# Three edits in the state-space rounds of a one-core hybrid trunk: where a second output row is scaled, how many rows the meta tokens' state product has, and which PSUM bank one output step uses

## The chip, the core and the metric

The kernel runs on one core of a Trainium2 chip. The metric is the device time of one execution in microseconds (us); lower is better. TensorE (PE in the profile, its weight loads PEld) multiplies matrices into PSUM, VectorE (DVE), ScalarE (ACT) and GpSimd (POOL) work element by element, SyncE (SP) issues transfers. Each engine runs its own list of instructions in the order of the list and waits on semaphores for what the others produce. PSUM has eight banks of 128 rows by 512 float32; a matmul writes into one of them.

## The reference

One layer of a hybrid decoder: RMS norm, one wide input projection, a pooling branch and a Mamba-2 branch, their gated sum, an output projection, an MLP and a final norm. 512 tokens are processed behind 16 learned meta tokens, with 1024 channels. The part that matters here is the Mamba-2 branch:

```python
xbc = jax.nn.silu(causal_depthwise_conv(xbc, conv_w, conv_b))     # x, B and C, width 4
dt = jax.nn.softplus(dt_raw + dt_bias);  a = -jnp.exp(a_log)
...
y_diag = jnp.einsum("bclsg,bclsgr,bcsgrp->bclgrp", cb, lmat, xdt)
states = jnp.einsum("bclgn,bclgr,bclgrp->bcgrpn", bf, decay_states, xdt)
...                                                               # states carried from chunk to chunk
y_off = jnp.einsum("bclgn,bcgrpn,bclgr->bclgrp", cf, prev, jnp.exp(a_cs))
y = (y_diag + y_off) + xs * d_skip[:, None]
y = y.reshape(bsz, seqlen, D_INNER) * jax.nn.silu(z)
yg = yg * lax.rsqrt(jnp.mean(yg * yg, axis=-1, keepdims=True) + EPS)   # over each of 8 groups
y_ssd = (yg * norm_w) @ w_ssd_out
```

The 16 meta tokens are a chunk of their own in front of four chunks of 128 tokens. There are 8 groups of 4 heads, 64 channels per head and 128 states.

## The kernel before

Everything is kept transposed: channels lie on the 128 partitions, tokens along the free axis. A float32 product is made of three float32r products (high by high, high by low, low by high), so each weight block of 128x1024 is loaded by SP, copied to a high half `whi` on ACT (L75) and its rest `wlo` taken on DVE (L76). Activations such as the branch's output are split in the same way, into `yh` (ACT, L542) and `yl` (DVE, L543).

The Mamba-2 branch runs in eight rounds g = 0 to 7, one per group. In a round the scan of group g (class `Scan`) is interleaved with four "steps" of PE work that keep TensorE filled (`scan_with`, L601 to L638). In rounds 0 to 3, 5 and 6 the steps are the projections of the next group: the B tile, the C tile and the two x tiles (`xbc_tile`), each followed by its convolution (`conv`, L344: one ACT instruction L347 and three DVE instructions L350). In round 4 they are the first half of the output projection (`out_half`), in round 7 its second part (`out_part`, L593): eight products `psp0` to `psp7` of six k-tiles each, added to `acc` by DVE (L597). The order inside the rounds is the order of the code for PE, ACT and DVE (`tc.manual_schedule`, L640); the program sets the waits.

A round, in the order of the code: `turn` transposes B and x on PE (tiles `ptb`, `ptx`, `ptm`) and forms `btok`, `xdt`, `xdd` and the meta tokens' operands `bm` and `xm`; then the step of PE work and its convolution; `spread` (ACT, L457: `eb`); `states` (PE: `pcb`, `pst`; ACT: `st` L486; DVE: `cbm`, `st` L488 and L489); second step; `spans` and `decays` (ACT, L463 and L468 on `abc`); third step; `spans`, `decays`, `scores` (DVE, L493); `outputs` (PE: `po` L503, `py` L509); then `gather`, `squares`, `norm`, `root` and `finish`, which scales the group's output rows by the norm and splits them.

Three places are touched.

*Second rows.* `finish` handles two rows of 128 channels. Where no gate product follows the round (rounds 0 and 5), the second row of group g is left for the next round: `rows.append(sc)`, and `scan_with` does it after the B tile's convolution and `spread` (L608). So it stands in rounds 1 and 6 only. Its three instructions are the multiply `yt` (DVE, L539), the cast `yh` (ACT, L542) and the rest `yl` (DVE, L543).

*Meta rows.* `bm` and `xm` hold the high parts, the rests and again the high parts at partitions 0, 32 and 64, with zeros between, in tiles of `MQ` = 80 partitions that are zeroed once (L140, L142). One float32r matmul over 80 rows (L485) is the meta chunk's state.

*PSUM.* Of the eight banks, four make up two double tiles (`psum2`, two buffers, used by projections and the output steps) and four are single tiles (`psum1`). In round 7 the first step is two products in a row (`two`, L644), both in double tiles. Ahead of them the two double buffers held `pz7` and the gate product `pgp6`; ACT reads `pgp6` for the sigmoid `m1` (L674), which was put in `held` and is issued after `turn`.

## Time and profile before

| | |
|---|---|
| median of three runs | 1012.45 us (1012.41 to 1012.48) |
| the profiled execution, its own time | 1012.34 us |
| its span, first to last instruction | 1010.5 us |
| PE / PEld busy | 999.8 us (99%) / 871.5 us (86%) |
| DVE busy | 712.3 us (70%) |
| ACT busy | 560.6 us (55%) |
| POOL busy | 88.7 us (9%) |
| granted TensorE clock | 0.999 |
| rounds 0 to 7 of the branch | about 66 to 475 us of the span |

Times in rows are us from the span's start, then the duration in us, the engine, the line, the operation and its tiles (out<-in), shapes and the number of merged instructions; a bracket gives the time the engine stood idle before it and who ended that. In a list of waits the columns are the total in us, how often, and the longest. The hardware pipelines instructions, so a row may begin some hundredths before the row ahead of it has ended. Buffer numbers are left out of tile names.

### The profile page before, as it was taken

To read this page: it belongs to the slowest core of one execution; us is meant where nothing else is said; L and a number is where in the kernel's file an instruction comes from. 1 tells how busy PE (TensorE), PEld (TensorE's weight loads), DVE (VectorE), ACT (ScalarE), POOL (GpSimd) and SP (SyncE) were. 2 spreads that over 40 slices of the span, in tenths; PEclk is the share of its full clock that TensorE was granted. 3 is DMA by queue.
4 is the path that set the end of the run, shared out by engine and by line. 5 is a ranking of instruction groups with operands and counts; after the bars stand their busy time and mean duration, and the time that the engine had idled before them with its cause. 6 is when DMAs were issued, how large, how long until landed. Compare 5 with 4: busy or idle time off the path is not lost.

```text
span 1010.5 us, 14027 instructions
## 1 busy us (share of the span) xinstructions
PE 999.8 (99%) x5689; PEld 871.5 (86%) x5689; DVE 712.3 (70%) x894; ACT 560.6 (55%) x789; POOL 88.7 (9%) x52
## 2 busy tenths in 40 slices
PE   9999999999999999999999999999999999999997
PEld 8889989898889999888898888888888888888886
DVE  7978687776745677677766557885766677666866
ACT  7756958595843659574244333465545455354444
POOL 0100000000000000000000001003040431412400
PEclk9999999999999999999999999999999999999999
DMA  6232232323232232324533234042323323324112
GB/s 242 71 142 104 64 125 84 120 73 131 75 127 90 76 119 70 132 78 133 179 105 95 94 104 177 10 161 90 104 91 117 104 84 125 104 84 126 42 42 84
DMA packets 29281, 105.62 MB, mean 105 GB/s; under 512 B 3296, under 2 KB 4256, under 8 KB 28192
## 3 DMA queue, kind: packets, MB, share of 16 engines
q1 hardware_dynamic: 26496, 92.75, 27.1%
q0 software_dynamic: 2000, 11.08, 2.8%
q8 instruction: 44, 0.72, 0.3%
q10 hardware_dynamic: 720, 0.91, 0.3%
q14 instruction: 21, 0.17, 0.1%
HBM read 102.55 MB, written 2.16 MB: 104 GB/s over the span
## 4 chain that ended last, share of the span: by engine, by line
PE 84%; DVE 7%; ACT 7%; issue 1%; DMA 0%; SPq 0%; DVEq 0%; ACTq 0%
PE pf L99 6%; PE pf L100 6%; PE pf L101 6%; PE px L157 3%; PE px L158 3%; PE px L160 3%; PE alpha L1071 3%; PE alpha L1072 3%; PE alpha L1073 3%; PE pz L160 2%; PE pz L157 2%; PE pz L158 2%; PE pp L157 2%; PE pp L160 2%; PE pp L158 2%; PE pso L99 1%
## 5 line engine op out<-in xcount | busy, mean ns | idle before, releaser
L76 DVE TENSOR_TENSOR wlo<-raw,whi 128x1024 fp32r<-128x1024 f32 (+1 forms) x131 | 163.9, 1252 | 111.8 <-ACT whi L75 111.5
L75 ACT CAST whi<-raw 128x1024 fp32r<-128x1024 f32 (+1 forms) x131 | 135.9, 1040 | 124.0 <-PE pf L100 55.7
L157 PE MATMUL px<-uh,whi 128*128 128x264 f32 (+1 forms) x448 | 118.9, 286 | 0.0
L158 PE MATMUL px<-ul,whi 128*128 128x264 f32 (+1 forms) x448 | 117.5, 283 | 0.0
L99 PE MATMUL pf<-vh,whi 128*128 128x512 f32 x256 | 99.8, 390 | 0.0
L101 PE MATMUL pf<-vh,wlo 128*128 128x512 f32 x256 | 99.6, 389 | 0.0
L100 PE MATMUL pf<-vl,whi 128*128 128x512 f32 x256 | 99.6, 389 | 0.0
L160 PE MATMUL px<-uh,wlo 128*128 128x264 f32 (+1 forms) x448 | 90.4, 283 | 0.0
L157 PEld LDWEIGHTS px<-uh,whi 128*128 128x128 f32 x448 | 84.8, 189 | 1.3 <-issue 1.0
L158 PEld LDWEIGHTS px<-ul,whi 128*128 128x128 f32 x448 | 84.4, 188 | 0.0
L833 DVE TENSOR_TENSOR slo<-b,shi 128x1024 fp32r<-128x1024 f32 x35 | 49.2, 1405 | 31.6 <-ACT shi L832 27.4
L160 PEld LDWEIGHTS px<-uh,wlo 128*128 128x128 f32 x448 | 68.8, 188 | 0.0
L832 ACT CAST shi<-b 128x1024 fp32r<-128x1024 f32 x35 | 36.8, 1050 | 47.3 <-PE pf L100 36.4
L101 PEld LDWEIGHTS pf<-vh,wlo 128*128 128x128 f32 x256 | 48.1, 188 | 10.1
L99 PEld LDWEIGHTS pf<-vh,whi 128*128 128x128 f32 x256 | 48.1, 188 | 9.9
L100 PEld LDWEIGHTS pf<-vl,whi 128*128 128x128 f32 x256 | 48.1, 188 | 9.9
L1082 POOL TENSOR_TENSOR b<-b,b 128x1024 f32<-128x1024 f32 x14 | 35.6, 2541 | 238.3 <-DVE slo L833 238.3
L1071 PE MATMUL alpha<-shi,hh 128*128 128x512 f32 x140 | 54.6, 390 | 0.0
L1073 PE MATMUL alpha<-shi,hl 128*128 128x512 f32 x140 | 54.5, 389 | 0.0
L1072 PE MATMUL alpha<-slo,hh 128*128 128x512 f32 x140 | 54.5, 389 | 0.0
L898 DVE TENSOR_TENSOR ht<-ht,alpha 128x1024 f32<-128x1024 f32 x35 | 42.6, 1217 | 10.9 <-PE alpha L1073 10.9
L157 PE MATMUL pz<-uh,whi 128*128 128x512 f32 x112 | 43.7, 390 | 0.0
(418 smaller groups left out, 2476.6 us busy)
## 6 DMA issues: line engine op xcount, KB each, us to landing
raw<-in_w SPq DMA_DIRECT2D x129, 512.0 KB, 3.5
b<-in_w SPq DMA_DIRECT2D x28, 512.0 KB, 3.5
abc<-acs_d POOLq DMA_DIRECT2D x8, 1024.0 KB, 5.3
wob<-in_w SPq DMA_DIRECT2D x8, 512.0 KB, 5.0
xt<-in_xT SPq DMA_DIRECT2D x8, 264.0 KB, 5.1
ht<-in_x POOLq DMA_DIRECT2D x4, 512.0 KB, 7.2
w<-in_w SPq DMA_DIRECT2D x4, 512.0 KB, 3.5
out_dram<-out SPq DMA_DIRECT2D x4, 320.0 KB, 2.4
```

Of the source, the lines that this page charges most:

```text
L75: act.copy(hi[:, c], raw[:, c])
L76: dve.tensor_tensor(lo[:, c], raw[:, c], hi[:, c].bitcast(F32), op=ALU.subtract)
L99: pe.matmul(ps, ah, bh, start=first, stop=False)
L100: pe.matmul(ps, ah, bl, start=False, stop=False)
L101: pe.matmul(ps, al, bh, start=False, stop=last)
L157: pe.matmul(o, wh, rhs[0][k][:, c], start=k == 0, stop=False)
L158: pe.matmul(o, wh, rhs[1][k][:, c], start=False, stop=False)
L160: pe.matmul(o, wl, rhs[0][k][:, c], start=False, stop=k == NK - 1)
L833: dve.tensor_tensor(lo, src, hi.bitcast(F32), op=ALU.subtract)
L1071: pe.matmul(ps[t], a[0], wh[:, cs], start=f, stop=False, skip_group_check=True)
L1072: pe.matmul(ps[t], a[0], wl[:, cs], start=False, stop=False, skip_group_check=True)
L1073: pe.matmul(ps[t], a[1], wh[:, cs], start=False, stop=l, skip_group_check=True)
```

## The change

`finish` is taken apart into `scale` (the multiply on DVE and the cast on ACT) and `rest` (the subtraction on DVE). In `scan_with` the scale of a left-over second row goes ahead of the convolution of the first step's tile; its rest stays where all three were. `bm` and `xm` are 128 partitions high, all of them zeroed once, and the product of L485 (L484 in the changed file) runs over 128 rows. In round 7 `psp1` is a single-bank tile.

```diff
-    bm = gc.tile([MQ, P], F32R, name="bm", bufs=1)
-    xm = gc.tile([MQ, R, HEAD], F32R, name="xm", bufs=1)
-    dve.tensor_scalar(bm, ones_f[:MQ], 0.0, None, op0=ALU.mult)
+    bm = gc.tile([P, P], F32R, name="bm", bufs=1)
+    xm = gc.tile([P, R, HEAD], F32R, name="xm", bufs=1)
+    dve.tensor_scalar(bm, ones_f, 0.0, None, op0=ALU.mult)
...
+        def scale(self, i):
+            y = self.yt[:, i, :]
+            dve.scalar_tensor_tensor(y, y, col(V_SN, 2 * self.g + i), self.rs, op0=ALU.mult, op1=ALU.mult)
+            self.yh = yp.tile([P, SEQ], F32R, tag="yh", name=f"yh{self.g}_{i}")
+            act.copy(self.yh, y)
+
+        def rest(self, i):
+            yl = yp.tile([P, SEQ], F32R, tag="yl", name=f"yl{self.g}_{i}")
+            dve.tensor_tensor(yl, self.yt[:, i, :], self.yh.bitcast(F32), op=ALU.subtract)
+            ys.append((self.yh, yl))
+
         def finish(self, tiles=(0, 1)):
             for i in tiles:
-                y = self.yt[:, i, :]
-                dve.scalar_tensor_tensor(y, y, col(V_SN, 2 * self.g + i), self.rs, op0=ALU.mult, op1=ALU.mult)
-                yh = yp.tile([P, SEQ], F32R, tag="yh", name=f"yh{self.g}_{i}")
-                yl = yp.tile([P, SEQ], F32R, tag="yl", name=f"yl{self.g}_{i}")
-                act.copy(yh, y)
-                dve.tensor_tensor(yl, y, yh.bitcast(F32), op=ALU.subtract)
-                ys.append((yh, yl))
+                self.scale(i)
+                self.rest(i)
...
-    def out_part(d):
-        ps = psum2(f"psp{d}")[:, :SEQ]
+    def out_part(d, psum=psum2):
+        ps = psum(f"psp{d}")[:, :SEQ]
...
         after = steps[0]()
+        if rows:
+            rows[0].scale(1)
         after()
         sc.spread()
-        while rows:
-            rows.pop().finish((1,))
+        if rows:
+            rows.pop().rest(1)
...
-                    return out_part(1)
+                    return out_part(1, psum1)
```

The changed program has the same instructions as the one before; these are the places where their order or their waits differ. On ACT in round 6 (round 1 is alike), from the rounding of the weight block that the B step prepared to the next block's; `yh5_1` is the second row's cast, `bt7` the B tile's convolution, `eb6` the spread, `st0_6` the meta state. Before:

```order
L75 CAST whi59_3904<-raw59_3903 128x1024 [waits DMAHW5_49]
L347 ACTIVATE bt7_3865<-px7_23_3902,vs_85 128x528 [waits PE_49]
L457 ACT_TABLE_LOAD
L457 ACTIVATE eb6_3961<-abc6_3862 64x1024 [waits DMASW2_49]
L457 ACTIVATE eb6_3961<-abc6_3862 64x1024
L542 CAST yh5_1_3965<-yt5_3684 128x512 [waits DVE_49]
L486 COPY st0_6_3976<-pst6_0_3980 128x256 [waits PE_49]
L75 CAST whi60_3995<-raw60_3994 128x1024 [waits DMAHW6_49]
```

In the changed program:

```order
L74 CAST whi59_3904<-raw59_3903 128x1024 [waits DMAHW5_49]
L539 CAST yh5_1_3958<-yt5_3684 128x512 [waits DVE_49]
L346 ACTIVATE bt7_3865<-px7_23_3902,vs_85 128x528 [waits PE_49]
L456 ACT_TABLE_LOAD
L456 ACTIVATE eb6_3964<-abc6_3862 64x1024 [waits DMASW2_49]
L456 ACTIVATE eb6_3964<-abc6_3862 64x1024
L485 COPY st0_6_3976<-pst6_0_3980 128x256 [waits PE_49]
L74 CAST whi60_3995<-raw60_3994 128x1024 [waits DMAHW6_49]
```

The cast, with its wait for DVE, moved from behind the spread to ahead of the convolution's first instruction. On DVE at the same place, from the rest of the same weight block to the first product of the states. Before:

```order
L76 TENSOR_TENSOR wlo59_3905<-raw59_3903,whi59_3904 128x1024 [waits DMAHW5_49,Activation_49]
L350 SCALAR_TENSOR_TENSOR bt7_3865<-px7_23_3902,vs_85,bt7_3865 128x527 [waits Activation_49]
L350 SCALAR_TENSOR_TENSOR bt7_3865<-px7_23_3902,vs_85,bt7_3865 128x526 [waits DVE_49]
L350 SCALAR_TENSOR_TENSOR bt7_3865<-px7_23_3902,vs_85,bt7_3865 128x525 [waits DVE_49]
L539 SCALAR_TENSOR_TENSOR yt5_3684<-yt5_3684,vs_85,rs5_3854 128x512
L543 TENSOR_TENSOR yl5_1_3966<-yt5_3684,yh5_1_3965 128x512 [waits Activation_49]
L477 TENSOR_TENSOR cbm6_3974<-pcb6_3969,tri_78 128x512 [waits PE_49]
L488 TENSOR_TENSOR st1_6_3977<-st0_6_3976,cdec_90 128x256 [waits Activation_49]
```

In the changed program:

```order
L75 TENSOR_TENSOR wlo59_3905<-raw59_3903,whi59_3904 128x1024 [waits DMAHW5_49,Activation_49]
L537 SCALAR_TENSOR_TENSOR yt5_3684<-yt5_3684,vs_85,rs5_3854 128x512
L349 SCALAR_TENSOR_TENSOR bt7_3865<-px7_23_3902,vs_85,bt7_3865 128x527 [waits Activation_49]
L349 SCALAR_TENSOR_TENSOR bt7_3865<-px7_23_3902,vs_85,bt7_3865 128x526 [waits DVE_49]
L349 SCALAR_TENSOR_TENSOR bt7_3865<-px7_23_3902,vs_85,bt7_3865 128x525 [waits DVE_49]
L543 TENSOR_TENSOR yl5_1_3967<-yt5_3684,yh5_1_3958 128x512
L476 TENSOR_TENSOR cbm6_3974<-pcb6_3969,tri_78 128x512 [waits PE_49]
L487 TENSOR_TENSOR st1_6_3977<-st0_6_3976,cdec_90 128x256 [waits Activation_49]
```

The multiply moved ahead of the three convolution instructions, but stays behind the weight block's rest. On PE in round 7, from the last k-tile of `psp0` into `psp1`. Before:

```order
L99 MATMUL psp0_4382<-yh6_1_4342,whi64_4269 128x512 [waits Activation_49]
L100 MATMUL psp0_4382<-yl6_1_4343,whi64_4269 128x512 [waits DVE_49]
L101 MATMUL psp0_4382<-yh6_1_4342,wlo64_4270 128x512
L99 MATMUL psp1_4408<-yh4_0_3111,whi64_4269 128x512 [waits Activation_49]
L100 MATMUL psp1_4408<-yl4_0_3112,whi64_4269 128x512
```

In the changed program:

```order
L98 MATMUL psp0_4382<-yh6_1_4342,whi64_4269 128x512 [waits Activation_49]
L99 MATMUL psp0_4382<-yl6_1_4344,whi64_4269 128x512 [waits DVE_49]
L100 MATMUL psp0_4382<-yh6_1_4342,wlo64_4270 128x512
L98 MATMUL psp1_4408<-yh4_0_3111,whi64_4269 128x512 [waits DVE_49]
L99 MATMUL psp1_4408<-yl4_0_3113,whi64_4269 128x512
```

`psp1` waited for ACT (the sigmoid that reads `pgp6`); now it waits for DVE, by its value for the first of the two `xdt` products of round 7, which is the last reader of `ptx7_0`, the single-bank tile whose buffer it takes over.

More of the change, by code (lines that the diff above doesn't have):

```diff
@@ L47 @@
 WARM = 9
-MQ = 80
 @with_exitstack
@@ L137 @@
     gc = gc_stack.enter_context(tc.tile_pool(name="gc", bufs=2, side="left", reuse_waits="tile"))
-    bm = gc.tile([MQ, P], F32R, name="bm", bufs=1)
-    xm = gc.tile([MQ, R, HEAD], F32R, name="xm", bufs=1)
-    dve.tensor_scalar(bm, ones_f[:MQ], 0.0, None, op0=ALU.mult)
+    bm = gc.tile([P, P], F32R, name="bm", bufs=1)
+    xm = gc.tile([P, R, HEAD], F32R, name="xm", bufs=1)
+    dve.tensor_scalar(bm, ones_f, 0.0, None, op0=ALU.mult)
     for i in range(2):
-        dve.tensor_scalar(xm[:, 2 * i : 2 * i + 2, :].rearrange("p r d -> p (r d)"), ones_f[:MQ], 0.0, None,
+        dve.tensor_scalar(xm[:, 2 * i : 2 * i + 2, :].rearrange("p r d -> p (r d)"), ones_f, 0.0, None,
                           op0=ALU.mult)
```

## The prediction

> **What bounds the kernel now.** I began with the page's busy shares and then read the list of what PE waited for.

> ```profile
> PE 999.8 (99%) x5689; PEld 871.5 (86%) x5689; DVE 712.3 (70%) x894; ACT 560.6 (55%) x789; POOL 88.7 (9%) x52
> PE py L509 <- ACT abc L468: 1.5, 2, 0.8
> PE pdt L201 <- DVE ones_r L109: 1.5, 1, 1.5
> PE psp L99 <- ACT m L674: 1.2, 1, 1.2
> PE pt_dt L319 <- DVE ddt L308: 0.3, 1, 0.3
> ```

> PE is busy for 99% of the span, and all its waits together are 4.5 us. So the time is PE's list of matmuls plus those waits: an edit counts only if it shortens or lengthens one of them, and what PE loses at a wait it never gets back. Two entries concern this change: `py` (two waits, 1.5 us) and `psp` (one, 1.2 us). The timeline of PE places them. Here are the two `py` waits with the last x-tile start ahead of the second, and the end of `psp0` with the start of `psp1`:

> ```profile
> 132.29 2.18 PE L509 MATMUL py<-abc,xdt 128*64 128x128 f32 x32 [0.75 <-ACT abc L468]
> 396.12 0.28 PE L157 MATMUL px<-uh,whi 128*128 128x264 f32 x1
> 404.64 2.18 PE L509 MATMUL py<-abc,xdt 128*64 128x128 f32 x32 [0.77 <-ACT abc L468]
> 434.69 0.39 PE L100 MATMUL psp<-yl,whi 128*128 128x512 f32 x1
> 434.92 0.39 PE L101 MATMUL psp<-yh,wlo 128*128 128x512 f32 x1
> 436.51 0.50 PE L99 MATMUL psp<-yh,whi 128*128 128x512 f32 x1 [1.21 <-ACT m L674]
> 436.85 0.39 PE L100 MATMUL psp<-yl,whi 128*128 128x512 f32 x1
> ```

> The `py` waits are in rounds 1 and 6, the only two rounds with a left-over second row. The third is in round 7, at the tile that changes its bank. All three lie where the change acts.

> What ends the `py` wait? By the waits in the program `py` needs DVE's first score product, which stands behind the C tile's convolution, which stands behind ACT's list. ACT in round 6, from the weight block's rounding on:

> ```profile
> 388.13 1.03 ACT L75 CAST whi<-raw 128x1024 fp32r<-128x1024 f32 x1
> 389.06 0.80 ACT L347 ACTIVATE bt<-px,vs 128x528 f32<-128x528 f32 x1
> ...
> 393.96 0.62 ACT L542 CAST yh<-yt 128x512 fp32r<-128x512 f32 x1 [0.65 <-DVE yt L539]
> ...
> 394.75 1.05 ACT L75 CAST whi<-raw 128x1024 fp32r<-128x1024 f32 x1
> ...
> 399.15 0.76 ACT L347 ACTIVATE ct<-px,vs 128x512 f32<-128x512 f32 x1
> ```

> and DVE beside it:

> ```profile
> 389.76 1.23 DVE L76 TENSOR_TENSOR wlo<-raw,whi 128x1024 fp32r<-128x1024 f32 x1
> 390.91 2.36 DVE L350 SCALAR_TENSOR_TENSOR bt<-px,vs,bt 128x527 f32<-128x527 f32 x3
> 393.18 0.74 DVE L539 SCALAR_TENSOR_TENSOR yt<-yt,vs,rs 128x512 f32<-128x512 f32 x1
> 394.61 0.69 DVE L543 TENSOR_TENSOR yl<-yt,yh 128x512 fp32r<-128x512 f32 x1 [0.69 <-ACT yh L542]
> ...
> 399.95 2.33 DVE L350 SCALAR_TENSOR_TENSOR ct<-px,vs,ct 128x512 f32<-128x512 f32 x3
> ...
> 403.32 2.36 DVE L493 TENSOR_TENSOR abc<-abc,cbm 128x1024 f32<-128x1024 f32 x2
> ```

> Read from the end: two score products start at 403.32, the first is done after half of 2.36 us, at about 404.5, and `py` starts at 404.64. (The profile puts the wait down to ACT's exponent L468, which ends a little earlier.) The scores follow the C tile's convolution, which starts at 399.95, the moment after ACT's share of it ends (399.15 + 0.76 = 399.91). From 394.75 to there ACT's rows have no idle time. So ACT's list in round 6 sets the `py` wait; each us by which ACT is late there is a us of PE.

> **The second row.** The change moves DVE's multiply ahead of three convolution products and ACT's cast ahead of the convolution's first instruction. The intention one can see is to use up ACT's 0.65 us and DVE's 0.69 us of idle time around the old cast. But ACT comes to the cast's new place when the rounding row of 388.13 is through, at about 389.1. DVE comes to the multiply only when its weight rest is through: that rest stays in front and starts at 389.76, so the multiply starts where the convolution started, at 390.91. ACT works in the order of its list, so it stands still for some 2.6 us with the convolution, the spread, the state copy and the next weight block queued behind it; that convolution had started at 389.06 without a wait before (its row has no bracket). The new time of the chain, step by step, with the handover and the pitches of round 6's first row and of a round without a second row (round 2):

> ```profile
> 384.48 0.62 ACT L542 CAST yh<-yt 128x512 fp32r<-128x512 f32 x1 [0.82 <-DVE yt L539]
> 385.00 0.47 ACT L428 COPY btok<-ptb 128x384 f32<-128x384 f32 x1
> 164.94 0.79 ACT L347 ACTIVATE bt<-px,vs 128x528 f32<-128x528 f32 x1
> 169.61 1.05 ACT L75 CAST whi<-raw 128x1024 fp32r<-128x1024 f32 x1
> ```

> - multiply at 390.91; the cast followed the multiply by 393.96 - 393.18 = 0.78 us: cast at 391.69;
> - the instruction behind a cast follows by 385.00 - 384.48 = 0.52 us: B's convolution on ACT at 392.21, where it was at 389.06;
> - from there to the next weight block with no cast between, as in round 2, 169.61 - 164.94 = 4.67 us: 396.88, where it was at 394.75.

> So ACT is **2.13 us** late from the weight block on, and C's convolution (402.08), the scores (405.45) and `py` (406.77) with it. Does DVE hold it longer? Its B convolution would run from about 393.05 to 395.41. From the old multiply to C's convolution DVE took 399.95 - 393.18 = 6.8 us, of which 0.7 were the multiply and 0.7 the wait for the cast; both are gone there, a wait of some 0.3 us for the late state copy comes in, so DVE stands ready at 395.4 + 5.4 + 0.3 = 401.1, ahead of 402.08: ACT decides. And the first x tile, which needs B's PSUM buffer, starts at 396.12 after 395.41: 0.7 us to spare. Nothing else PE runs before `py` needs the late work. Round 1 has the same rows:

> ```profile
> 116.72 0.80 ACT L347 ACTIVATE bt<-px,vs 128x528 f32<-128x528 f32 x1
> 117.42 1.23 DVE L76 TENSOR_TENSOR wlo<-raw,whi 128x1024 fp32r<-128x1024 f32 x1
> 120.85 0.74 DVE L539 SCALAR_TENSOR_TENSOR yt<-yt,vs,rs 128x512 f32<-128x512 f32 x1
> 122.41 1.06 ACT L75 CAST whi<-raw 128x1024 fp32r<-128x1024 f32 x1
> ```

> DVE's pitch of 1.15 us (390.91 - 389.76) puts the multiply at 118.57, the cast at 119.35, the convolution at 119.87, the next block at 124.54 against 122.41: 2.13 us again. The waits of PE go from 0.75 and 0.77 to about 2.9 us each. **Term: +4.25 us.** Lower end: ACT loses only the new idle time less the old, 2 x (2.6 - 0.65) = 3.9. Upper end: every handover a little longer than read, 4.4.

> The earlier `yh` and `yl` help nobody: those rows are first read in round 4 and in round 7.

> **The PSUM bank.** `psp1` has waited for the sigmoid on ACT. Without a wait it would start one step after the last row of `psp0`, at 434.92 + 0.23 = 435.15; it started at 436.51, and its successor 0.34 instead of 0.23 us later: 1.36 + 0.11 = 1.47 us. What is late next? The new wait is for the first of two DVE products, and three later matmuls wait for the turned tiles:

> ```profile
> 434.31 1.28 DVE L437 TENSOR_TENSOR xdt<-ptx,dtok 128x512 f32<-128x512 f32 x2
> 438.01 0.28 DVE L450 TENSOR_TENSOR bm<-ptb,bm 16x128 fp32r<-16x128 f32 x1
> 441.63 1.46 PE L483 MATMUL pst<-xdd,btok 128*128 128x256 f32 x6
> 443.05 0.40 PE L99 MATMUL psp<-yh,whi 128*128 128x512 f32 x1
> 443.25 0.37 ACT L486 COPY st<-pst 128x256 f32<-128x256 f32 x1 [1.45 <-PE pst L485]
> ```

> The first DVE product ends half of 1.28 us after 434.31, at 434.95, some 0.2 us before it is needed; only the early load of the weights may come a little late. With PE 1.4 us earlier the states' products would come at 440.2, still behind the last piece of `bm` (438.29) whose bank one of them takes over. ACT's copy of the meta state waits for PE and moves with it. `psp2` now takes the sigmoid's buffer, free at 436.5, long before 441.6. DVE's wait at the round's first state shrinks and its later work keeps ahead of `py`. **Term: -1.4 us**, from -1.3 to -1.47.

> **The meta rows.** The matmul over 80 rows takes 0.47 us (below) where one over 128 rows takes 0.28 (396.12 above), which looks like a price for 80 rows. But its row overlaps the states' products ahead of it: their six records end at 441.63 + 1.46 = 443.09, the meta product ends at 443.21, 0.12 us later, and 0.12 is also what a second projection matmul adds to a first (0.40 for two against 0.28 for one). And 88 rows elsewhere cost nothing extra:

> ```profile
> 24.16 0.41 PE L276 MATMUL pb<-dgh,ones_r 88*128 88x264 f32 x2
> 442.74 0.47 PE L485 MATMUL pst<-xm,bm 80*128 80x256 f32 x1
> 398.78 0.40 PE L160 MATMUL px<-uh,wlo 128*128 128x264 f32 x2
> ```

> Two of 88 rows and 264 columns take 0.41, two of 128 rows take 0.40. The zeroing covers more partitions in the same instructions, once, at the very start. **Term: 0**; the outer bound below is 8 x (0.31 - 0.12) = -1.5 us, if the step from 442.74 to 443.05 were all the rows' doing; above, I see none.

> **The sum.** 4.25 - 1.4 = +2.85 us. The profiled execution took 1012.34 us, 1.84 of them outside its span of 1010.50; its span becomes 1013.35 and its time 1015.19. The median of the runs is 0.11 us above it: **1015.3 us**, +0.28%.

> **The rivals.**

> *ACT does not stand still (faster).* If the multiply were done when ACT reaches the cast, the idle 0.65 us around the old cast would go, the two `py` waits with it, and round 7's gain would come on top: 1012.45 - 1.5 - 1.4 = 1009.5 us. The point from which it decides: DVE would have to be free for the multiply by about 388.3. Against it: DVE has no idle time ahead of its weight rest at 389.76. 8%.

> *One wait grows only.* If one of the two rounds hid its lag, +2.13 - 1.4: 1013.2 us. The rows of rounds 1 and 6 agree to 0.02 us, which speaks against it. 5%.

> *The meta rows did cost.* With -1.5 us besides, 1013.8 us. The 88-row matmuls speak against it. 6%.

> *The clock falls in the longer waits.* Two waits of 2.9 us are the longest idle times of PE after its first microseconds; so far 1.2 us is the longest, and the clock row of the page shows 9 in every slice. What a slow clock would cost is seen at the start:

> ```profile
> 1.51 3.78 PE L201 MATMUL pdt<-ones_r 128*128 128x512 f32 x9 [1.51 <-DVE ones_r L109]
> ```

> Nine matmuls of 512 columns take 0.42 us each there, against 0.23 in round 7: 1.7 us lost over such a stretch. Behind both waits that is 3.4 us more: 1018.7 us. 6%. [...]

> *The bank comes free late.* If `psp1` had to wait for the last piece of `bm` instead (438.29), its wait would be 3.2 us where it was 1.36: 1.8 us more and no gain, 1012.45 + 4.25 + 1.8 = 1018.5 us. The program's wait speaks against it. 3%.

> **How the numbers follow.** The forecast has the remaining 72%; its own range is 3.9 - 1.47 to 4.4 - 1.3, +2.4 to +3.1, so 1014.9 to 1015.6. The range for 8 in 10 adds the two cases at 1013.2 and 1013.8 (83% together) and some room above: 1013.2 to 1016.2. A measurement of this kernel tells 0.2% (2.0 us) from no change. Slower: forecast, clock and late bank, 81%; same: the one-wait and meta cases, 11%; faster: 8%.

> **What would show it.** In rounds 1 and 6 ACT's cast directly behind the weight rounding with about 2.6 us of idle time before it, ended by DVE's multiply; the next weight block 2.1 us later after B's first matmul than before; `py` waits near 2.9 us each; no wait at `psp1`; meta products with the same step; the clock unchanged. I am wrong if the two `py` waits shrink, if `psp1` still waits, or if a wait appears that is in no list here.

## The result and the profile after

| | before | after |
|---|---|---|
| median of six runs each | 1012.47 us (1012.32 to 1012.85) | 1017.25 us (1016.61 to 1018.28) |
| ratio to before | | 1.0048 (1.0035 to 1.0061) |
| the profiled execution / its span | 1012.34 / 1010.5 us | 1017.60 / 1015.9 us |
| granted TensorE clock of that execution | 0.999 | 0.996 |

The change costs 4.8 us, where 2.85 were forecast: the direction was right, the time lies 1.95 us above the forecast and 1.05 above the range. The six runs of the changed kernel scatter by 1.7 us, those of before by 0.5, and their order is that of their clock: 1016.61 us at 0.998, 1016.87 and 1016.90 at 0.997, 1017.60 and 1017.99 at 0.996, 1018.28 at 0.995. Of the executions below, one of the kernel with the single bank alone took 1244.72 us at a clock of 0.752 and is left out of its median and ratio, and the profiled one of the kernel with five filling products had a mean clock of 0.949 (1016.23 us), so its rows are not used.

The page's busy shares and the list of what PE waited for, of the changed kernel (total us, times, longest):

```profile
PE 1002.1 (99%) x5689; PEld 874.3 (86%) x5689; DVE 712.5 (70%) x894; ACT 560.7 (55%) x789; POOL 88.7 (9%) x52
PE py L508 <- ACT abc L467: 5.8, 2, 2.9
PE pdt L200 <- DVE ones_r L108: 1.5, 1, 1.5
PE pt_dt L318 <- DVE ddt L307: 0.3, 1, 0.3
PE pdt L157 <- DVE xl L208: 0.2, 1, 0.2
```

The `py` waits went from 1.5 to 5.8 us and the wait of `psp` is gone, as forecast. Those two entries make +4.3 and -1.2. But PE's busy time rose too, from 999.8 to 1002.1 us, with the same 5689 matmuls. That is the part that the sum had no term for. PE's timeline (start, duration) of the changed kernel shows where:

```profile
134.54 3.41 PE L508 MATMUL py<-abc,xdt 128*64 128x128 f32 x32 [2.87 <-ACT abc L467]
137.88 0.39 PE L156 MATMUL px<-uh,whi 128*128 128x264 f32 x1
...
410.22 3.35 PE L508 MATMUL py<-abc,xdt 128*64 128x128 f32 x32 [2.88 <-ACT abc L467]
413.50 0.59 PE L156 MATMUL px<-uh,whi 128*128 128x264 f32 x1
...
441.88 0.39 PE L100 MATMUL psp<-yh,wlo 128*128 128x512 f32 x1
442.11 0.40 PE L98 MATMUL psp<-yh,whi 128*128 128x512 f32 x1
```

and of the kernel before, the x-tile matmuls that follow `py`:

```profile
134.41 0.39 PE L157 MATMUL px<-uh,whi 128*128 128x264 f32 x1
...
406.76 0.39 PE L157 MATMUL px<-uh,whi 128*128 128x264 f32 x1
```

The 32 products of `py` took 2.18 us before and take 3.41 and 3.35 us after. The windows view around both waits gives the reason (stretch, its us, then the busy time of each engine with its count, the granted clock, the DMA share, GB/s):

```profile
131.70:134.60 2.90, 0.06 (x2) 0.09 (x3) 2.90 (x4) 2.87 (x7) 0.00 (x0) 0.92 0.06 24
134.60:137.50 2.90, 2.90 (x28) 2.90 (x30) 2.83 (x4) 1.20 (x2) 0.00 (x0) 0.50 0.43 158
137.50:140.50 3.00, 3.00 (x29) 2.83 (x26) 2.86 (x5) 0.00 (x0) 0.53 (x1) 0.99 0.34 139
407.40:410.30 2.90, 0.08 (x2) 0.11 (x4) 2.90 (x4) 2.87 (x7) 0.00 (x0) 1.00 0.06 23
410.30:413.20 2.90, 2.90 (x32) 2.86 (x32) 2.83 (x4) 1.17 (x2) 0.00 (x0) 0.55 0.44 164
413.20:414.20 1.00, 1.00 (x8) 0.71 (x5) 1.00 (x2) 0.00 (x0) 0.34 (x1) 0.59 0.00 0
414.20:417.00 2.80, 2.80 (x26) 2.80 (x25) 2.62 (x5) 0.00 (x0) 0.19 (x1) 1.00 0.69 284
```

The column to read is the number behind POOL's bracket: 1.00 is full speed. During the first wait it is 0.92 (the fall begins in its last half us), during the second 1.00; behind both it is 0.50 to 0.59, and about 3 us later 0.99 and 1.00 again. The record of clock changes in the same trace has two stretches at half clock ahead of the program's end, each of 3.413 us; by the windows they begin at 134.13 and 410.61. So PE stood still for 2.87 us, and then worked for the next 3 us at half the clock.

The starts of the same matmuls in both timelines give the size of each step ("of which new" is what a row adds to the lateness of the row above it):

| PE starts | before | after | later by | of which new |
|---|---|---|---|---|
| `po`, round 1 | 129.60 | 129.72 | 0.12 | 0.12, from the start of the program |
| `py`, round 1 | 132.29 | 134.54 | 2.25 | 2.13, the wait |
| first `px` behind it | 134.41 | 137.88 | 3.47 | 1.22, the clock |
| `po`, round 6 | 401.93 | 405.39 | 3.46 | 0 |
| `py`, round 6 | 404.64 | 410.22 | 5.58 | 2.12, the wait |
| third `px` behind it | 407.10 | 414.07 | 6.97 | 1.39, the clock |
| last matmul of `psp0` | 434.92 | 441.88 | 6.96 | 0 |
| second matmul of `psp1` | 436.85 | 442.34 | 5.49 | -1.47, the bank |
| end of the span | 1010.5 | 1015.9 | 5.4 | -0.1 |

On the engines that cause the wait, the order is the forecast one. ACT in round 6:

```profile
391.58 1.04 ACT L74 CAST whi<-raw 128x1024 fp32r<-128x1024 f32 x1
395.14 0.62 ACT L539 CAST yh<-yt 128x512 fp32r<-128x512 f32 x1 [2.52 <-DVE yt L537]
395.67 0.79 ACT L346 ACTIVATE bt<-px,vs 128x528 f32<-128x528 f32 x1
...
400.33 1.05 ACT L74 CAST whi<-raw 128x1024 fp32r<-128x1024 f32 x1
...
404.73 0.76 ACT L346 ACTIVATE ct<-px,vs 128x512 f32<-128x512 f32 x1
```

and DVE:

```profile
393.22 1.23 DVE L75 TENSOR_TENSOR wlo<-raw,whi 128x1024 fp32r<-128x1024 f32 x1
394.36 0.75 DVE L537 SCALAR_TENSOR_TENSOR yt<-yt,vs,rs 128x512 f32<-128x512 f32 x1
396.49 2.36 DVE L349 SCALAR_TENSOR_TENSOR bt<-px,vs,bt 128x527 f32<-128x527 f32 x3 [1.38 <-ACT bt L346]
...
405.52 2.32 DVE L349 SCALAR_TENSOR_TENSOR ct<-px,vs,ct 128x512 f32<-128x512 f32 x3 [1.20 <-ACT ct L346]
```

The cast stands directly behind the weight's rounding and has 2.52 us of idle time before it, ended by DVE's multiply (2.6 forecast). From one weight rounding to the next ACT now takes 400.33 - 391.58 = 8.75 us, where it took 394.75 - 388.13 = 6.62: 2.13 us more, the forecast lag.

### The profile page after: what moved, and what is told of

Same layout as the page of the kernel before. It is cut to its first block, busy times and chain, and to the rows that moved or that the text cites. A ratio compares the mean times of both kernels' runs of the same rounds, so it can differ in the third digit from the quotient of the medians.

```text
span 1015.9 us, 14028 instructions
## 1 busy us (share of the span) xinstructions
PE 1002.1 (99%) x5689; PEld 874.3 (86%) x5689; DVE 712.5 (70%) x894; ACT 560.7 (55%) x789; POOL 88.7 (9%) x52
## 4 chain that ended last, share of the span: by engine, by line
PE 85%; ACT 7%; DVE 7%; issue 1%; DMA 0%; SPq 0%; DVEq 0%; ACTq 0%
PE pf L99 6%; PE pf L98 6%; PE pf L100 6%; PE px L156 3%; PE px L157 3%; PE px L159 3%; PE alpha L1078 3%; PE alpha L1079 3%; PE alpha L1080 3%; PE pz L159 2%; PE pz L156 2%; PE pz L157 2%; PE pp L156 2%; PE pp L159 2%; PE pp L157 2%; PE pso L98 1%
## 5 line engine op out<-in xcount | busy, mean ns | idle before, releaser
L75 DVE TENSOR_TENSOR wlo<-raw,whi 128x1024 fp32r<-128x1024 f32 (+1 forms) x131 | 163.9, 1253 | 114.0 <-ACT whi L74 113.7
L157 PE MATMUL px<-ul,whi 128*128 128x264 f32 (+1 forms) x448 | 117.4, 283 | 0.0
L100 PE MATMUL pf<-vh,wlo 128*128 128x512 f32 x256 | 99.6, 389 | 0.0
L99 PE MATMUL pf<-vl,whi 128*128 128x512 f32 x256 | 99.6, 389 | 0.0
L157 PEld LDWEIGHTS px<-ul,whi 128*128 128x128 f32 x448 | 84.6, 189 | 0.0
L100 PEld LDWEIGHTS pf<-vh,wlo 128*128 128x128 f32 x256 | 48.0, 188 | 10.0
L99 PEld LDWEIGHTS pf<-vl,whi 128*128 128x128 f32 x256 | 48.1, 188 | 9.9
```

The costliest lines, as they stand in the source:

```text
L75: dve.tensor_tensor(lo[:, c], raw[:, c], hi[:, c].bitcast(F32), op=ALU.subtract)
L99: pe.matmul(ps, ah, bl, start=False, stop=False)
L100: pe.matmul(ps, al, bh, start=False, stop=last)
L157: pe.matmul(o, wh, rhs[1][k][:, c], start=False, stop=False)
```

## The experiments

Three theories stood against each other for the surplus. The clock theory: PE's clock falls after the long waits, and what it loses is the surplus. Its rivals: one of the other two parts costs something after all; or the moved work gets in the way of something else, with the clock only a sign of it. The runs of before that stood beside the experiments had medians from 1012.39 to 1012.62 us, and the ratios are against these.

### Which part it is

The second row put back behind `spread`; the 128 rows and the single bank stay:

```diff
         after = steps[0]()
-        if rows:
-            rows[0].scale(1)
         after()
         sc.spread()
         if rows:
+            rows[0].scale(1)
             rows.pop().rest(1)
```

> The changed kernel with the second row's multiply and cast put back behind the spread; the 128 meta rows and the single bank stay. Theory A (the cast makes ACT 2.13 us late in rounds 1 and 6, and each of the two waits of 2.88 us that PE gets from it halves the TensorE clock for a stretch, 1.2 to 1.4 us each): both effects go, the clock stays at 0.999, the waits at py are 0.75 and 0.77 again and only the bank's gain is left: 1012.45 - 1.45 = 1011.0 us. Theory B (a part of the 5 us comes from the bank or the meta rows): above 1011.5 us.

Measured: 1011.02 us, ratio 0.9986 (0.9977 to 0.9995). PE's waits of this kernel:

```profile
PE py L508 <- ACT abc L467: 1.5, 2, 0.8
```

The two waits are back at their old size, the clock is 0.999, and what is left is the gain of the bank.

The kernel before with the second row's move alone (80 meta rows, `psp1` in a double tile):

> The kernel before with the second row's multiply and cast moved, and nothing else: 80 meta rows and psp1 in a double tile. Theory A: the waits at py are 2.88 us, the clock falls behind both, psp1 keeps its wait of 1.2 us: the changed kernel's 1017.25 + 1.45 = 1018.7 us. Theory B (bank or meta rows add to the slowdown): at or under 1017.2 us.

Measured: 1019.61 us, ratio 1.0072 (1.0059 to 1.0084). So the move of the row alone holds the loss and more: 0.9 us above the 1018.7 forecast. Its rows say something that was not expected. The two `py` blocks on PE with the `po` block of round 6, and the windows behind them:

```profile
134.86 3.68 PE L508 MATMUL py<-abc,xdt 128*64 128x128 f32 x32 [2.86 <-ACT abc L467]
...
407.07 1.95 PE L502 MATMUL po<-ct,st 128*128 128x128 f32 x16
411.91 2.18 PE L508 MATMUL py<-abc,xdt 128*64 128x128 f32 x32 [2.89 <-ACT abc L467]
```

```profile
134.90:138.30 3.40, 3.40 (x32) 3.24 (x32) 3.33 (x5) 1.22 (x2) 0.00 (x0) 0.50 0.39 147
138.30:141.70 3.40, 3.40 (x21) 3.23 (x18) 3.23 (x5) 0.00 (x0) 0.53 (x1) 0.63 0.37 152
412.00:415.40 3.40, 3.40 (x43) 3.00 (x44) 3.33 (x5) 1.17 (x2) 0.53 (x1) 1.00 0.37 140
```

Both waits are as long as in the changed kernel (2.86 and 2.89 us). In round 6 the clock did not fall at all, and `py` took its 2.18 us. In round 1 it stayed low for 6.827 us, twice 3.413, so the second of these windows still shows 0.63. The cost of that one fall comes from the starts, as in the table above: `py` of round 1 is 134.86 - 132.29 = 2.57 us later than before, `po` of round 6 407.07 - 401.93 = 5.14, so 2.57 us were lost between them. (Of the first 2.57, 2.12 are the lag; 0.45 are there already at `po` of round 1, at 130.05 against 129.60; the trace's first record of full clock begins at 7.72 us of the span, that of the kernel before at 4.64.) The length of the wait alone does not decide what it costs; the last experiments come back to that.

The kernel before with `MQ = 128` in place of 80, and nothing else:

> The kernel before with 128 meta rows and nothing else. The prediction's reading (the 0.47 us row of the meta product is an overlap, its own step is 0.12 us): no change, 1012.45 us, within 0.2 us, the row still 0.47 us. Rival (80 rows cost 0.19 us in each of eight rounds): 1.5 us less, 1011.0 us, the row near 0.28 us.

Measured: 1012.75 us, ratio 1.0002 (0.9993 to 1.0010). The meta product's row, by source line, in this kernel (duration in ns, lowest, median and highest; first and last start):

```profile
L485 PE MATMUL pst<-xm,bm x8: 469/469/469, 76.0 to 443.2; 128*128 128x256 f32 x8
```

It was 470 ns with 80 rows. The rows are worth nothing that these runs can show, and the rival's 1.5 us lie outside the interval.

The kernel before with `psp1` in a single bank, and nothing else:

```diff
-                    return out_part(1)
+                    return out_part(1, psum1)
```

> The kernel before with psp1 in a single bank and nothing else. The prediction's term: 1.45 us less, 1011.0 us, and the wait at psp1 gone from PE's list while the two at py stay at 0.75 and 0.77 us. Rival (part of the gain is given back at a later wait in round 7): 1011.3 us or more, with a wait in the round's po or py.

Measured: 1011.14 us (median of eleven runs), ratio 0.9983 (0.9975 to 0.9992), 1.48 us less than the 1012.62 of before beside it; the `psp` entry is gone from PE's waits, the `py` entry is unchanged at 1.5 us, and no wait at `po` has come in. With these four runs the rivals that blame the meta rows or the bank are gone: the loss belongs to the second row.

### Whether it is the clock

If the clock falls because PE stands still, then giving PE anything to do in the wait must save time, although it does more work. In the changed kernel twelve products of the constant ones are put ahead of `py` in rounds 1 and 6; they write `py`'s own bank, and `py`'s first product overwrites them:

```diff
+            if g in (1, 6):
+                for _ in range(12):
+                    pe.matmul(self.py[0].rearrange("p (a b) -> p a b", a=4), ones_r,
+                              ones_r.unsqueeze(1).to_broadcast([P, 4, P]), start=True, stop=True)
```

> The changed kernel with twelve matmuls of 128x512 of ones more in rounds 1 and 6, written into py's own bank between po and py, where they are overwritten; at 0.227 us each they fill 2.7 of the 2.88 us for which PE waits. Every chain of ACT and DVE stays as late as in the changed kernel. Theory A (the clock is what adds to the lag): the clock stays near 0.999, py takes 2.18 us again, and the time is the lag and the bank alone, 1012.45 + 4.25 - 1.45 = 1015.2 us, 2.0 to 2.6 us under the changed kernel although it does more. Theory B (py is slowed by something else in these rounds, such as the weight loads that move at the same time): py stays at 3.4 us and the time at 1017 us.

Measured: 1015.27 us (1015.12 to 1015.41), ratio 1.0025 (1.0015 to 1.0036). PE's rows and the windows of round 1:

```profile
131.55 3.02 PE L506 MATMUL py<-ones_r 128*128 128x512 f32 x12
134.69 2.18 PE L512 MATMUL py<-abc,xdt 128*64 128x128 f32 x32
```

```profile
131.50:134.60 3.10, 3.06 (x15) 2.20 (x13) 3.06 (x5) 3.07 (x8) 0.00 (x0) 1.00 0.22 52
134.60:138.00 3.40, 3.31 (x42) 2.93 (x43) 3.33 (x5) 1.36 (x2) 0.53 (x1) 1.00 0.39 145
```

The clock is 1.00 in both windows and `py` is back at 2.18 us. `py` starts at 134.69, no earlier than the 134.54 of the changed kernel: the lag is still there in full. Yet the kernel is 2.0 us faster and scatters by 0.3 us. The kernel with the row alone is the test from the other side: in its round 6 the same moved work and a wait of 2.89 us came without a fall of the clock, and `py` took 2.18 us there too. So the clock is the cause of the surplus, not a sign of it. And without the falls the time is 1015.27 us, where 1015.3 were forecast.

### How long PE must stand still

The same edit with fewer products leaves PE idle for a part of the wait: three leave 2.17 us, seven 1.24, five some 1.7 (an estimate: 2.17 less two products at 0.23).

> The changed kernel with three filling matmuls instead of twelve in rounds 1 and 6: 0.7 of the 2.9 us are filled, and PE then stands idle for about 2.1 us without a break. The chains are as late as before, so the time is 1015.2 us if the clock stays. Theory A1 (the gate looks at stretches of 3.4 us and halves the clock only where PE was idle for most of one, some 2.5 us or more): 0.999 and 1015.2 us in all runs. Theory A2 (a wait between 1.2 and 2.1 us is enough, seen or not according to where the stretch begins): the runs scatter between 1015.2 and 1018 us, the clock of the profile below 0.999.

> The same with seven filling matmuls: 1.6 us filled, some 1.3 us idle, about as long as psp1's wait of 1.2 us in the kernel before, which left the clock alone. Theories A1 and A2: 0.999 and 1015.2 us in all runs. If the clock fell here too, it would follow the lateness of the chains and not the idle time: 1016 to 1018 us.

> The changed kernel with five filling matmuls in rounds 1 and 6, between the seven that kept the clock (1.25 us idle) and the three that did not (2.17 us idle, 1015.1 to 1018.6 us): about 1.7 us idle without a break, half of the 3.4 us for which the clock stays low once it falls. Theory A2a (the gate compares the share of idle time in a stretch of 3.4 us with about a half): at the edge, most runs at 1015.2 us, few above. Theory A2b (it needs two thirds or so): all runs at 1015.2 us. Theory A2c (a third is enough): runs scatter up to 1018 us as with three.

Three products: 1017.68 us, ratio 1.0047 (1.0035 to 1.0059). The five runs lie between 1015.09 at clock 0.999 and 1018.55 at 0.995; four of them above 1017.4. The profiled one has both falls:

```profile
134.96 3.07 PE L512 MATMUL py<-abc,xdt 128*64 128x128 f32 x32 [2.17 <-ACT abc L467]
...
410.79 2.87 PE L512 MATMUL py<-abc,xdt 128*64 128x128 f32 x32 [2.18 <-ACT abc L467]
```

Seven: 1015.13 us, ratio 1.0025 (1.0015 to 1.0034), nine runs from 1014.70 to 1015.57, `py` at 2.18 us. Five: 1015.16 us, ratio 1.0028 (1.0017 to 1.0039), six runs from 1015.02 to 1015.20. So by their times 2.17 us of idle time still bring the fall in most runs, 1.7 us in none of six.

Is it the longest unbroken idle time, or the idle time in sum? Three products that wait for the weight's rest on DVE fall into the middle of the wait and cut it in two:

```diff
+            if g in (1, 6):
+                for _ in range(3):
+                    pe.matmul(self.py[0], ones_r, ahead[-1][3][:, :SEQ], start=True, stop=True)
```

> The changed kernel with three filling matmuls as in the run with 2.17 us idle, but these three read the weight rest that DVE finishes in the middle of the wait, so that they run there: the same 0.7 us of work and the same idle time in sum, 2.2 us, in two pieces of about 1.7 and 0.5 us. Theory U (an unbroken idle time of more than some 1.7 us lets the clock fall): 1015.2 us or as with five. Theory S (the idle time in sum over a stretch counts): the runs scatter up to 1018.5 us as with three in front.

Measured: 1016.24 us, ratio 1.0035 (1.0021 to 1.0049), five runs from 1015.49 at clock 0.999 to 1016.70 at 0.998. PE in the profiled one:

```profile
133.76 0.97 PE L506 MATMUL py<-wlo,ones_r 128*128 128x512 f32 x3 [1.68 <-DVE wlo L75]
134.94 2.18 PE L511 MATMUL py<-abc,xdt 128*64 128x128 f32 x32 [0.22 <-issue]
...
408.20 0.97 PE L506 MATMUL py<-wlo,ones_r 128*128 128x512 f32 x3 [1.69 <-DVE wlo L75]
409.38 3.58 PE L511 MATMUL py<-abc,xdt 128*64 128x128 f32 x32 [0.21 <-issue]
```

Pieces of 1.69 and 0.21 us brought a fall in round 6, though 1.7 us in one piece brought none in the runs with five products; nearly the same pieces in round 1 brought none. That speaks for the sum (which came to 1.9 us here, not the 2.2 expected), and for a second condition that differs between two alike waits.

The second condition can be read from the clock records. In the changed kernel and in that with three products (falls at 135.65 and 412.13 us) the two falls begin 276.48 us apart, which is 81 times 3.4133 us, although their waits end 275.68 and 275.83 us apart. The other changes fit the same step: from the start of the first record of full clock to the first fall it is 129.71 us in the changed kernel, 38 times 3.4133, and from the start of that record to the fall at the program's end 1003.52 us in the kernel before, 294 times. That first record itself begins anywhere from 4.42 us (the changed kernel) to 7.72 us (the row alone) of the span. So in these records the changes sit on a grid of 3.41 us, which the waits did not shift. With the grid of each trace laid over its waits (the falls of the row alone and of the wait cut in two begin at 134.01 and 409.30), the idle time that fell into one stretch of the grid was:

| kernel, round | wait on PE | idle in the fullest stretch | clock in the next stretch |
|---|---|---|---|
| changed, 6 | 2.88 us | 2.88 us | half |
| changed, 1 | 2.87 | 2.46 | half |
| three products, 1 | 2.17 | 2.17 | half |
| three products, 6 | 2.18 | 2.07 | half |
| row alone, 1 | 2.86 | 2.01 | half |
| wait cut in two, 6 | 1.69 + 0.21 | 1.82 | half |
| row alone, 6 | 2.89 | 1.47 | full |
| wait cut in two, 1 | 1.68 + 0.22 | 1.16 | full |

(Row alone, round 6: the stretch from 407.08 to 410.49 holds the idle time from 409.02 on, 1.47 us, and the next one the rest, 1.42.) The eight cases part cleanly between 1.47 and 1.82 us, about half of the stretch, 1.71; seven products (1.25 at most) and before (1.21 at most, at `psp1`) agree. That the wait's length alone does not decide is shown by the two waits of 2.86 and 2.89 us in one execution; that the share of one stretch of the grid decides, and that half is the limit, is an inference from these ten or so waits. It would also explain the scatter: with a wait of 2.2 to 2.9 us, where the grid happens to lie would decide whether a run pays for no, one or two falls. One execution of each kernel has a trace, so for the other runs this rests on their times and mean clocks. Nor is all scatter of this kind: 24 runs of the kernel before beside the experiments took from 1011.86 to 1014.34 us, all at a clock of 0.998 or more.

### A version that beats both

The multiply early, as in the change, since DVE has room there; the cast back behind `spread`, where ACT no longer has to wait for it:

```diff
         def scale(self, i):
             y = self.yt[:, i, :]
             dve.scalar_tensor_tensor(y, y, col(V_SN, 2 * self.g + i), self.rs, op0=ALU.mult, op1=ALU.mult)
+
+        def cast(self, i):
             self.yh = yp.tile([P, SEQ], F32R, tag="yh", name=f"yh{self.g}_{i}")
-            act.copy(self.yh, y)
+            act.copy(self.yh, self.yt[:, i, :])
...
         sc.spread()
         if rows:
+            rows[0].cast(1)
             rows.pop().rest(1)
```

> The changed kernel with the second row's multiply ahead of B's convolution as there, but its cast on ACT back behind the spread, so that the multiply is long done when ACT comes to the cast. Theory A (only the place of the cast on ACT's list does harm): ACT's 0.65 us of idle time ahead of the cast goes, PE's two waits at py shrink from 0.76 to about 0.1 us, no wait above 0.5 us is left in the rounds, the clock stays at 0.999: 1012.45 - 1.45 - 1.3 = 1009.7 us, faster than both kernels. Theory B (the multiply ahead of the convolution itself makes DVE late, 0.6 us): the waits stay or grow to about 1.4 us: 1011.0 to 1012.3 us.

Measured: 1009.71 us, ratio 0.9974 (0.9965 to 0.9983). ACT's cast and the multiply on DVE:

```profile
393.99 0.62 ACT L541 CAST yh<-yt 128x512 fp32r<-128x512 f32 x1
```

```profile
391.56 0.74 DVE L537 SCALAR_TENSOR_TENSOR yt<-yt,vs,rs 128x512 f32<-128x512 f32 x1
```

The cast has no bracket: no idle time. PE's list of waits has neither `py` nor `psp` left, only entries of the first microseconds. Against the first experiment, which differs only in the place of the multiply, it saves 1.31 us of the 1.5 that the two `py` waits took.

## Why the prediction was wrong, point by point

**What bounds the kernel** held: PE's matmuls and its waits make the time, and each part acted through a wait of PE. What the sum left out is that the same matmuls can take longer: the 32 products of `py` went from 2.18 to 3.41 and 3.35 us.

**The second row.** Right in mechanism and size. The lag was 2.13 us in round 1 and 2.12 in round 6, each forecast at 2.13; the waits are 2.87 and 2.88 us, forecast near 2.9.

**The PSUM bank.** Right: -1.47 us in the changed kernel, -1.48 by itself, forecast -1.4 with an end at -1.47.

**The meta rows.** Right: no time that the runs can show (1012.75 against 1012.62 us), and the product's 0.47 us is not its own step, as the overlap of its row with the rows ahead of it suggested.

**The step that failed** is the sum: 4.25 - 1.4 had no term for the clock behind the two lengthened waits, and the runs showed one of 2.6 us. The prediction had put the clock among the rivals, with "clock unchanged" as what would show the forecast right. The rival was named with its place and cause, priced at 1.7 us for each wait, and given 6%; the range ended 2.5 us below its 1018.7. It came true in both rounds of the profiled execution, at 1.22 and 1.39 us, 2.6 us in all. Added to the forecast of 1015.19 that is 1017.8, and the profiled execution took 1017.60. The price was too high because part of a low stretch lies in the wait itself (in round 1 from 134.13 to 134.54) and because `py` does not slow by the full factor of two: its 2.18 us became 3.41.

What misled was the reading of the bound. The trace of before had no wait of PE between 1.2 us, behind which the clock stayed at 1.00, and what the change would make, 2.9. The cost over that gap should have been bounded from both sides; here it was left out of the forecast, though no row of that trace showed that a wait of 2.9 us leaves the clock alone. The runs showed that it need not: half clock followed 2.88, 2.17 and even 1.9 us of idle time. With both ends kept, 0 and 3.4 us, the range would have reached 1018.7 and held the result.

**The other rivals.** That ACT does not stand still did not come true, but its time of 1009.5 us was sound: the version with the cast left behind reaches 1009.71. One wait growing only, the meta rows' cost and a late bank are all excluded by the rows above.

## What to carry to other kernels

A step moved "into idle time" must be early on the engine that produces its input, not only on the one that runs it: the multiply had room ahead of the convolution, the cast behind it on ACT did not, and moving only the first gains where moving both loses. When an edit lengthens a wait of PE beyond any that the trace shows, count the work behind it at both clocks, and look at the granted clock of that stretch before looking for more waits. If such a wait can't be removed, filling it with products that nobody reads may win back the clock; here that was worth 2.0 us.
